# A diffusion layer on one core: context values and the bias on ScalarE's queue, value stores a step late, router sums over eight units

## The chip, the cores and the metric

The kernel runs on one core of one Trainium2 chip. The metric is the device time of one execution in microseconds (us), as the median over runs. The core has five engines that work side by side, each through its own list of instructions in order: TensorE (PE, its weight loads listed as PEld), VectorE (DVE), ScalarE (ACT), GpSimd (POOL) and SyncE (SP). SP does nothing but ask for transfers. In this kernel nearly all transfers are asked for on SP's queue; the other engines' queues can do it too, and then the requests stand in order among that engine's own instructions.

## What is computed

One layer for 1024 latent tokens of width 1024 and 256 context tokens. The input projection feeds three groups of heads: neighbourhood attention (8 heads of 64), a two-way linear recurrence (LRU, 256 channels) and a gated short convolution (256 channels). Each group is normalised, all go through one output projection, and a mixture of 16 experts follows.

```python
...
u = h @ w_in
uc = hc @ w_in[:, c_lo:c_hi]
...
# neighbourhood attention, one row of the grid, 4 groups of 16 queries, 8 rows x 32 columns of keys and the context
s_loc = jnp.einsum('bnqhd,brnkhd->bhnqrk', qr, kb) * scale + bias     # masked to the window
s_ctx = jnp.einsum('bnqhd,bchd->bhnqc', qr, kc) * scale
p = jax.nn.softmax(jnp.concatenate([s_loc, s_ctx], -1), axis=-1)
out = p_loc @ vb + p_ctx @ vc
...
y = jnp.concatenate([rms_norm(y_na, g0), rms_norm(y_lru, g1), rms_norm(y_sc, g2)], -1) @ w_out
x = x + mod[:, 2] * y
h = modulate(rms_norm(x, norm_ffn_g), mod[:, 3], mod[:, 4])
x = x + mod[:, 5] * moe_ffn(h)          # router: softmax(h @ w_router + b_router), top-2 within a group
return rms_norm(x, final_g)
```

`mod` are six rows of 1024 numbers, silu(c) @ w_ada + b_ada.

## The kernel before

All matrix products are made of two or three products of rounded parts: a number is split into a high and a low part (`hi` by a copy on ScalarE, `lo` by a subtraction on VectorE).

**Input projection** (`inproj`). The 22 blocks of 128 output columns are taken in the order of `CHUNKS`: LRU and convolution inputs, the gates, then values (blocks 10 to 13), keys (14 to 17) and queries (18 to 21). A block has two groups of 512 tokens, and blocks of keys, values and LRU inputs a third of 256 context tokens; a group is 24 matmuls (L334). Other work runs between them as Python generators in two lists, `side` and `late`: after the first half of a group `pump(side)` lets each task of `side` go on to its next `yield`, after the second half, `pump(side, late)` does it for both. A `yield` is thus the distance of one step, and what a task issues between two yields is written at that place into every engine's list. Tasks that the change touches:

- `norm` (L457 to L496), twice (convolution, then LRU): squares on ScalarE (L463), their sum on GpSimd (L464), two yields, then the sum over channels by matmuls with a column of ones into `pm` (L469), a root (L471, L472), a broadcast by matmuls (L478), scaling on VectorE (L482), splitting (L489 makes the low part) and four stores to `y_d` in device memory. `gelu` (L448 to L454) makes its input.
- `mod_rows` (from L504), four passes `p`, for the modulation rows 2 to 5: eight loads of `w_ada` (`mw`), summed on VectorE into `macc` (L518, then L520), a split (L526 on GpSimd makes the low part into `mw`), one yield, and four matmuls per pass with a column of ones (L532).
- `ev_v` for the values: it transposes a group's `vT` on PE (L622), copies the high part from PSUM into one of three buffers (L627, ScalarE), subtracts for the low part (L628, VectorE) and asks SP for the store to `v_d`.

**Attention** has 32 units `u` (4 column groups of 8 heads) of two halves `g`. Per half: scores by four matmuls (L760), bias addition and row maximum in one instruction on VectorE (L764), exponential (L772, ScalarE), five transposes (L783), a copy for the high part (L785) and a subtraction (L786) for the low part, then the value matmuls L810 of the unit before, over 13 jobs: 5 in the first half, 8 in the second. `vw[0..3]` are rows of the latent values (`block<-v_d`, `values_rows`), `vc` the context values. The bias tables `bt` (two buffers, for two heads each) come from `b_d` by two loads per pair of heads, then GpSimd adds the mask in two instructions (L723); `bias(p)` does pair `p`, with pair 0 before attention.

**Router weights.** `wout_step(u)` at u = 24 multiplies and sums eight columns of `wr` into `sws` (L958, then seven L960) and folds the row into `wr` (L961).

What orders the work: the order of the source lines, the two generator lists, and the order on SP's queue.

Of the kernel before, what the change touches and what calls it, by code (L numbers as in the profile page):

```python
# [8 lines left out]
F32 = mybir.dt.float32  # L9
# [9 lines left out]
P = 128  # L19
# [52 lines left out]
class Kernel:  # L72
# [291 lines left out]
    def inproj(self, hc_es):  # L364
# [93 lines left out]
        def norm(ys, base):  # L458
# [3 lines left out]
            for ch in range(2):  # L462
                S.activation(sq[ch][:, 0:T], ys[ch][:, 0:T], AF.Square)  # L463
            G.tensor_add(out=sq[0][:, 0:T], in0=sq[0][:, 0:T], in1=sq[1][:, 0:T])  # L464
            yield 1
            yield 1
            pn = self.pmm.tile([P, 8], F32, name="pm")
            for t in range(8):
                E.matmul(pn[:, t:t + 1], sq[0][:, t * P:(t + 1) * P], ones[:, 0:1], start=True, stop=True)  # L469
# [28 lines left out]
        def mod_rows():  # L498

            def get(q):  # L500
                if q < 4 * KD:
                    p, k = divmod(q, KD)
                    wa = self.mo.tile([P, D], F32, name="mw", bufs=2)
                    self.load(wa, a["w_ada"][k * P:(k + 1) * P, (p + 2) * D:(p + 3) * D])  # L504
                    was.append(wa)
            was = []
            get(0)
            one = self.mo.tile([P, 1], F32R, name="one", bufs=1)
            S.copy(one, ones[:, 0:1])
            for p in range(4):  # L510
                acc = self.mo.tile([P, D], F32, name="macc")
                row = self.mo.tile([1, D], F32, name="mrow")
                self.load(row, a["b_row"][:, (p + 2) * D:(p + 3) * D])
                for k in range(KD):
                    get(p * KD + k + 1)
                    wa = was.pop(0)
                    if k == 0:
                        V.tensor_scalar_mul(acc, wa, self.sil[:, 0:1])  # L518
                    else:
                        V.scalar_tensor_tensor(out=acc, in0=wa, scalar=self.sil[:, k:k + 1], in1=acc, op0=ALU.mult, op1=ALU.add)  # L520
                    if k != 1:
                        yield 1
                hi = self.vp.tile([P, D], F32R, name="mhi", bufs=1)
                S.copy(hi, acc)
                lo = self.mo.tile([P, D], F32R, name="mw", bufs=2)
                G.tensor_sub(out=lo, in0=acc, in1=hi.bitcast(F32))  # L526
                yield 1
                for hh in range(2):
                    cs = slice(hh * 512, hh * 512 + 512)
                    pr = self.psu.tile([P, 512], F32, name="ps")  # L530
                    for i, x in enumerate((hi, lo)):
                        E.matmul(pr[0:1, :], one, x[:, cs], start=(i == 0), stop=(i == 1))  # L532
                    V.tensor_add(row[:, cs], pr[0:1, :], row[:, cs])
                self.load(self.mod_d[p:p + 1, :], row)
                yield 1
# [76 lines left out]
            side.append(gelu(ch, x))  # L612
        side.append(norm(ylru, 0))

        def ev_v(ch):
            pend = []

            def transposes():
                o, n, vT = pend.pop()
                pt = self.pst.tile([P, 512], F32, name="pt")  # L620
                for i in range(n // P):
# [4 lines left out]
                pv = pt[:, 0:n].rearrange("p (b d) -> p b d", d=64)  # L626
                S.copy(vo[:, 0:2 * nb, 0, :], pv)  # L627
                V.tensor_sub(vo[:, 0:2 * nb, 1, :], pv, vo[:, 0:2 * nb, 0, :].bitcast(F32))  # L628
                self.load(self.v_d[o:o + n, 2 * ch:2 * ch + 2].rearrange("(b p) h j d -> p b (h j d)", p=P),
                          vo[:, 0:2 * nb].rearrange("p (b h) j d -> p b (h j d)", h=2).bitcast(F32))  # L630

            def ev(g, o, n, ps):
                if pend:
# [8 lines left out]
        for ch in range(4):  # L642
# [8 lines left out]
            block(10 + ch, evac)  # L651
            flush = fl
        flush()
        drain(side)
        gp_es.close()

# [56 lines left out]
        for g in range(2):  # L713
            self.load(self.masks[n][:, g], self.a["mask"][3 * g + TY[n]])

    def bias(self, p):

        n, h, bt = p // 4, 2 * (p % 4), self.bts[p % 2]
        for g in range(2):
            o = (128, 0)[g]  # L720
            v = bass.AP(tensor=bt.tensor, offset=bt[:, g, 0:1].offset, ap=[list(bt.ap[0]), [640, 2], [1, 384]])
            self.load(v, self.b_d[h:h + 2, TY[n], :, o:o + 384].rearrange("h p k -> p h k"))
            self.G.tensor_add(out=v, in0=v, in1=self.masks[n][:, g:g + 1].to_broadcast([P, 2, 384]))  # L723

    def values_rows(self, n, u):
# [8 lines left out]
    def attention(self):  # L734
# [9 lines left out]
        with self.pool("ap") as ap:  # L744
# [43 lines left out]
            def values(u, part):  # L788
                n, h = divmod(u, 8)
                vw = vws[n]  # L790
                if part == 0:
# [3 lines left out]

                jobs = [(vc[:, 0, h], 3, 3), (vc[:, 1, h], 4, 4), (vw[1][:, h], 1, 0), (vw[2][:, h], 2, 1),
                        (vw[0][:, h], 0, None), (vw[3][:, h], None, 2)]
                jobs = [(ph, P) + j for j in jobs[2:] + jobs[:1]] + [(pl, 64) + j for j in jobs] + [(ph, P) + jobs[1]]
                for q, (pp, m, w, b0, b1) in enumerate(jobs):
                    if (q >= 5) != part:  # L800
                        continue
# [52 lines left out]
                for j in range(2):  # L854
                    self.load(self.y_d[j][2 * n + g, :, 0:4], yn[j].bitcast(F32))

            self.load(vc.bitcast(F32), self.v_d[T:TA].rearrange("(b p) h j d -> p b h (j d)", p=P))
            self.bias(1)
            self.load(grow, a["mg"][:, 0:512].to_broadcast([P, 512]))
            last = 32  # L860
            for g in range(2):
# [43 lines left out]
    def wout_step(self, u):  # L905
# [36 lines left out]
        if u == 31:  # L942
# [8 lines left out]
            self.mix_load(1, [self.kq[i] for i in (12, 13, 14)])  # L951
            self.slot = op.tile([P, P], F32, name="slot")
            self.load(self.slot, a["slot"].to_broadcast([P, P]))
        if u == 24:
            V, cols, wr = self.V, self.cols, self.wr

            V.scalar_tensor_tensor(out=cols[1], in0=cols[1], scalar=1.0, in1=cols[2], op0=ALU.add, op1=ALU.mult)
            V.tensor_scalar_mul(self.sws, wr[:, 0, :], cols[0][:, 0:1])  # L958
            for k in range(1, KD):
                V.scalar_tensor_tensor(out=self.sws, in0=wr[:, k, :], scalar=cols[0][:, k:k + 1], in1=self.sws, op0=ALU.mult, op1=ALU.add)  # L960
            V.tensor_tensor(out=wr, in0=wr, in1=cols[1][:, :, None].to_broadcast([P, KD, NE]), op=ALU.mult)  # L961

    def mix_load(self, it, bufs=None):
# [871 lines left out]
```

## Time and profile before

| | us |
|---|---|
| median of 3 runs (lowest, highest) | 1130.27 (1129.08, 1131.17) |
| the profiled execution | 1134.46 |
| its span on the core | 1132.5 |
| PE busy | 1020.2 (90%) |
| PEld busy | 836.5 (74%) |
| VectorE busy | 825.3 (73%) |
| ScalarE busy | 592.1 (52%) |
| GpSimd busy | 307.9 (27%) |

251.21 MB move, 222 GB/s on average, and the mean granted clock is 0.96. The input projection lasts until about 392 us, attention until about 565, the output projection and the router until about 700, the experts until the end. A row of the timeline gives the start and the length, then engine, line, operation, what it writes and reads, shapes and count (several equal neighbours in one row), and in brackets how long the engine had been idle before it and what ended this. For SP the length is the time of asking, not that of the transfer.

### The profile page before, as it was taken

How to read it: one execution, taken by the hardware profiler on the slowest of the kernel's cores; microseconds unless marked ns; L12 is line 12 of the kernel's file. 1: busy time of each engine (PE TensorE's matmuls, PEld its weight loads, DVE VectorE, ACT ScalarE, POOL GpSimd, SP SyncE). 2: the span in 40 equal slices, each digit the busy share in tenths (PEclk: the TensorE clock that was granted, in tenths of full speed). 3: DMA queues.
4: the chain of work that ended last, by engine and by line, in shares of the span. 5: the costliest groups of instructions: out<-in, count | busy, mean ns of one | idle time of the engine just before them, and what ended most of it. 6: DMA issues, size and time to landing. Idle time of an engine off the chain costs nothing. (4 is left out here: it accounts for less than half of the span.)

```text
span 1132.5 us, 15754 instructions
## 1 busy us (share of the span) xinstructions
PE 1020.2 (90%) x5242; PEld 836.5 (74%) x5243; DVE 825.3 (73%) x1415; ACT 592.1 (52%) x964; POOL 307.9 (27%) x212
## 2 busy tenths in 40 slices
PE   2699999998999979998799997699999999999994
PEld 2587777786888779897678886577777777777773
DVE  5876898644553358887667776879898979788965
ACT  6565673431233258786522223556565757566751
POOL 3630011310001034344303224131423233231432
PEclk9879999998999989998999997899999999999997
DMA  9441434878624676774776856978989989898873
GB/s 330 125 121 60 133 96 116 277 259 258 208 85 116 146 217 179 213 213 129 266 249 215 295 156 228 343 275 251 337 271 310 289 274 323 242 350 241 300 242 138
DMA packets 139595, 251.21 MB, mean 222 GB/s; under 512 B 25283, under 2 KB 87205, under 8 KB 139460
## 3 DMA queue, kind: packets, MB, share of 16 engines
q1 hardware_dynamic: 131620, 229.97, 61.9%
q0 software_dynamic: 6736, 19.53, 7.4%
q8 instruction: 45, 0.74, 0.3%
q10 hardware_dynamic: 1152, 0.63, 0.2%
q14 instruction: 42, 0.34, 0.1%
HBM read 211.94 MB, written 45.55 MB: 227 GB/s over the span
## 5 line engine op out<-in xcount | busy, mean ns | idle before, releaser
L334 PE MATMUL ps<-h,block 128*128 128x512 f32 x1056 | 258.8, 403 | 2.8 <-DVE block L321 1.8
L334 PEld LDWEIGHTS ps<-h,block 128*128 128x128 f32 x1056 | 201.6, 194 | 45.0 <-DVE block L321 2.6
L1367 PE MATMUL pg<-q,xT 128*128 128x512 f32 x448 | 137.3, 399 | 3.4 <-DVE xT L93 2.7
L1367 PE MATMUL pg<-k,xT 128*128 128x512 f32 x320 | 113.2, 408 | 3.9 <-PEq L1578 3.7
L1323 POOL DMA_INDIRECT acc_d<-yt,recs x15 | 69.3, 4620 | 125.4 <-DVE yt L1392 125.4
L1367 PEld LDWEIGHTS pg<-q,xT 128*128 128x128 f32 x448 | 84.9, 190 | 24.6 <-DVE xT L93 2.8
L1743 DVE TENSOR_TENSOR q<-block,k 128x1024 fp32r<-128x1024 f32 x80 | 94.9, 1218 | 2.7 <-ACT k L1742 1.8
L1387 PE MATMUL py<-k,hT 128*128 128x512 f32 x204 | 81.1, 435 | 10.3 <-DVE hT L1379 4.2
L1742 ACT CAST k<-block 128x1024 fp32r<-128x1024 f32 x80 | 80.2, 1047 | 3.7 <-DMA recs<-list_d 3.4
L723 POOL TENSOR_TENSOR bt<-bt,mask 128x768 f32<-128x768 f32 x32 | 59.0, 1859 | 81.8 <-DMA bt<-b_d 61.1
L1367 PEld LDWEIGHTS pg<-k,xT 128*128 128x128 f32 x320 | 61.7, 193 | 18.5 <-issue 3.8
L772 ACT ACTIVATE sm<-sm,mx 128x640 f32<-128x640 f32 x64 | 53.2, 832 | 26.6 <-DVE mx L764 26.5
L786 DVE TENSOR_TENSOR p<-ps,p 128x640 fp32r<-128x640 f32 x64 | 52.6, 822 | 16.1 <-ACT p L785 16.1
L520 DVE SCALAR_TENSOR_TENSOR macc<-mw,sil,macc 128x1024 f32<-128x1024 f32 x28 | 40.7, 1455 | 28.4 <-DMA mw<-in_w_ada_dram 28.2
L783 PE MATMUL ps<-cst,sm 128*128 128x128 f32 x320 | 49.6, 289 | 12.9 <-DVE mx L764 12.0
L1387 PEld LDWEIGHTS py<-k,hT 128*128 128x128 f32 x204 | 39.6, 194 | 28.0 <-DVE hT L1379 10.7
L764 DVE CUSTOM_DVE_ANT_0 sm<-ps,bt 128x640 f32<-128x640 f32 x64 | 52.2, 818 | 9.9 <-POOL bt L723 7.1
L760 PE MATMUL ps<-k,q 128*128 128x384 f32 (+1 forms) x256 | 53.8, 335 | 4.0 <-DVE yn L93 2.3
L1284 POOL DMA_INDIRECT block<-h_d,recs x21 | 27.1, 1292 | 96.3 <-PE pt L1333 87.3
L785 ACT CAST p<-ps 128x640 fp32r<-128x640 f32 x64 | 44.3, 692 | 14.9 <-PE ps L783 14.4
L783 PEld LDWEIGHTS ps<-cst,sm 128*128 128x128 f32 x320 | 38.3, 149 | 16.0 <-issue 12.7
L760 PEld LDWEIGHTS ps<-k,q 128*128 128x128 f32 x256 | 44.6, 200 | 5.9 <-DVE yn L93 2.5
(373 smaller groups left out, 2293.9 us busy)
## 6 DMA issues: line engine op xcount, KB each, us to landing
block<-in_w_moe_dram SPq DMA_DIRECT2D x120, 512.0 KB
raw<-in_w_moe_dram SPq DMA_DIRECT2D x36, 512.0 KB
mw<-in_w_ada_dram SPq DMA_DIRECT2D x32, 512.0 KB
bt<-b_d SPq DMA_DIRECT2D x32, 384.0 KB
k<-in_w_moe_dram SPq DMA_DIRECT2D x24, 512.0 KB
block<-in_w_in_dram SPq DMA_DIRECT2D x22, 512.0 KB
wa<-in_w_ada_dram SPq DMA_DIRECT2D x16, 512.0 KB
block<-v_d SPq DMA_DIRECT2D x64, 128.0 KB
```

Source lines behind the costliest of these rows:

```text
L334: self.E.matmul(ps[:, 0:n], l[:, k, :], r[:, m, :], start=(k == 0 and q == 0), stop=(k == KD - 1 and q == 2))
L723: self.G.tensor_add(out=v, in0=v, in1=self.masks[n][:, g:g + 1].to_broadcast([P, 2, 384]))
L760: E.matmul(ps[:, dst], self.qs[i][h][:, it * P:(it + 1) * P], kv, start=(i == 0), stop=(i == 1))
L764: V.tensor_tensor_reduce(out=sm, in0=ps[:, all_], in1=self.bts[(u // 2) % 2][:, g, b0:b0 + 640], op0=ALU.add, op1=ALU.min, scale=-1.0, sca ...
L772: S.activation(sms[u, g], sms[u, g], AF.Exp, scale=-1.0, bias=mx, accum_out=lss[n][:, g, h:h + 1])
L783: E.transpose(pt[:, b * P:(b + 1) * P], sm[:, c:c + P], ident)
L786: return lambda: V.tensor_sub(pl, pt, ph.bitcast(F32))
L1323: nc.gpsimd.indirect_dma_start(out=acc_d, out_offset=bass.IndirectOffsetOnAxis(ap=rec[0:m, 1:2], axis=0), in_=y[0:m], in_offset=None, comp ...
L1367: E.matmul(self.pg[half], self.xT[x][:, k, :], self.w.gu(k, m, half), start=(k == 0 and i == 0), stop=(k == KD - 1 and i == 2))
L1387: E.matmul(self.py[c], hTs[x][:, f, :], self.w.dn(f, m, c), start=(f == 0 and i == 0), stop=(f == 3 and i == 2))
L1742: k.S.copy(hi, raw)
L1743: (eng or k.V).tensor_sub(lo, raw, hi.bitcast(F32))
```

## The change

Six edits:

1. `norm` has three yields, not two, ahead of the matmuls with ones.
2. `mod_rows` has one more yield between the split and the row matmuls, in each of four passes.
3. `ev_v` keeps a value store back in `done` and asks for it when the next tile has been copied; the last is asked for after the last tile.
4. At the start of attention, `bias(1)` is asked for first and then `vc`, both on ScalarE's queue; before, SP was asked for `vc`, then `bias(1)`.
5. The value jobs are in another order: the first half has the four latent ones with the high part and the first with the low part, the context ones all come in the second half.
6. The eight sums of `sws` are asked for one each in units 17 to 24; the two other instructions stay at u = 24.

Line numbers of the changed kernel are 1 larger from L527, and up to 13 larger behind.

```diff
@@ norm
-            yield 1
-            yield 1
+            for _ in range(3):
+                yield 1
@@ mod_rows
                 G.tensor_sub(out=lo, in0=acc, in1=hi.bitcast(F32))
                 yield 1
+                yield 1
@@ inproj
+        done = []
+
+        def store():
+
+            while done:
+                self.load(*done.pop())
+
@@ ev_v
-                self.load(self.v_d[o:o + n, 2 * ch:2 * ch + 2].rearrange("(b p) h j d -> p b (h j d)", p=P),
-                          vo[:, 0:2 * nb].rearrange("p (b h) j d -> p b (h j d)", h=2).bitcast(F32))
+                store()
+                done.append((self.v_d[o:o + n, 2 * ch:2 * ch + 2].rearrange("(b p) h j d -> p b (h j d)", p=P),
+                             vo[:, 0:2 * nb].rearrange("p (b h) j d -> p b (h j d)", h=2).bitcast(F32)))
@@ inproj, behind the blocks of values
         flush()
+        store()
@@ bias
-            self.load(v, self.b_d[h:h + 2, TY[n], :, o:o + 384].rearrange("h p k -> p h k"))
+            self.load(v, self.b_d[h:h + 2, TY[n], :, o:o + 384].rearrange("h p k -> p h k"), eng)
@@ values
-                jobs = [(ph, P) + j for j in jobs[2:] + jobs[:1]] + [(pl, 64) + j for j in jobs] + [(ph, P) + jobs[1]]
+                jobs = [(ph, P) + j for j in jobs[2:]] + [(pl, 64) + j for j in jobs[2:] + jobs[:2]] + [(ph, P) + j for j in jobs[:2]]
@@ attention
-            self.load(vc.bitcast(F32), self.v_d[T:TA].rearrange("(b p) h j d -> p b h (j d)", p=P))
-            self.bias(1)
+            self.bias(1, S)
+            self.load(vc.bitcast(F32), self.v_d[T:TA].rearrange("(b p) h j d -> p b h (j d)", p=P), S)
@@ wout_step
+        if 17 <= u < 25:
+            V, k, s = self.V, u - 17, self.cols[0][:, u - 17:u - 16]
+            if k == 0:
+                V.tensor_scalar_mul(self.sws, self.wr[:, k, :], s)
+            else:
+                V.scalar_tensor_tensor(out=self.sws, in0=self.wr[:, k, :], scalar=s, in1=self.sws, op0=ALU.mult, op1=ALU.add)
@@ wout_step, u == 24
-            V.tensor_scalar_mul(self.sws, wr[:, 0, :], cols[0][:, 0:1])
-            for k in range(1, KD):
-                V.scalar_tensor_tensor(out=self.sws, in0=wr[:, k, :], scalar=cols[0][:, k:k + 1], in1=self.sws, op0=ALU.mult, op1=ALU.add)
```

The first place at which the order on an engine differs is VectorE in the first block of values, while the LRU norm runs. `g_816`, `g_817` and `g_822` are tiles of values (L628 is L636 in the changed kernel), L482 and L489 the norm's, `macc` the modulation row, L321 a weight split. Before:

```order
L482 SCALAR_TENSOR_TENSOR g_823<-g_823,vt,ps 128x512
L482 SCALAR_TENSOR_TENSOR g_821<-g_821,vt,ps 128x512
L520 SCALAR_TENSOR_TENSOR macc<-mw,sil,macc 128x1024 x2
L489 TENSOR_TENSOR g_825<-g_823,g_818 128x8x4x16
L489 TENSOR_TENSOR g_819<-g_821,g_815 128x8x4x16
L628 TENSOR_TENSOR g_816<-pt,g_816 128x8x64
L520 SCALAR_TENSOR_TENSOR macc<-mw,sil,macc 128x1024
L628 TENSOR_TENSOR g_817<-pt,g_817 128x8x64
L520 SCALAR_TENSOR_TENSOR macc<-mw,sil,macc 128x1024
L321 SCALAR_TENSOR_TENSOR block_2005<-block_1872,block_2004 128x1024
L628 TENSOR_TENSOR g_822<-pt,g_822 128x4x64
```

On the same engine at the same place in the changed kernel:

```order
L482 SCALAR_TENSOR_TENSOR g_823<-g_823,vt,ps 128x512
L482 SCALAR_TENSOR_TENSOR g_821<-g_821,vt,ps 128x512
L636 TENSOR_TENSOR g_816<-pt,g_816 128x8x64
L489 TENSOR_TENSOR g_825<-g_823,g_818 128x8x4x16
L489 TENSOR_TENSOR g_819<-g_821,g_815 128x8x4x16
L518 TENSOR_SCALAR macc<-mw,sil 128x1024
L636 TENSOR_TENSOR g_817<-pt,g_817 128x8x64
L520 SCALAR_TENSOR_TENSOR macc<-mw,sil,macc 128x1024 x2
L321 SCALAR_TENSOR_TENSOR block_1998<-block_1852,block_1997 128x1024
L636 TENSOR_TENSOR g_822<-pt,g_822 128x4x64
```

The pair of L520 that stood between L482 and L489 is gone from there; the pass of the row begins (L518) behind L489, and a pair of L520 stands ahead of the third tile's subtraction.

The second place is the start of attention: SP before, from the last rows of values (`block_2900`) on, and ScalarE in the changed kernel. DMAHW0 to DMAHW7 are eight counters of finished transfers that all requests use in turn; a request waits until the one before it on its counter has landed. Before, on SP:

```order
L84 DMA block_2900<-v_d 32x1024 [waits DMAHW7_49]
L84 DMA q_2661<-q_2661 64x1024 [waits DMAHW0_49,Activation_49]
L84 DMA q_2669<-q_2669 64x1024 [waits DMAHW1_49,DVE_49]
L84 DMA q_2662<-q_2662 64x1024 [waits DMAHW2_49,Activation_49]
L84 DMA q_2670<-q_2670 64x1024 [waits DMAHW3_49,DVE_49]
L84 DMA vc<-v_d 128x2x1024 [waits DMAHW4_49,PE_49]
L84 DMA bt_2978<-b_d 128x2x384 [waits DMAHW5_49,PE_49]
L84 DMA bt_2978<-b_d 128x2x384 [waits DMAHW6_49]
L84 DMA grow<-in_mg_dram 128x512 [waits DMAHW7_49]
```

On ScalarE in the changed kernel, and, in the second fence, on SP:

```order
L702 CAST q_2661<-ps 64x8x4x16 [waits PE_49]
L702 CAST q_2662<-ps 64x8x4x16 [waits DVE_49]
L84 DMA bt_2978<-b_d 128x2x384 [waits DMAHW4_49]
L84 DMA bt_2978<-b_d 128x2x384 [waits DMAHW6_49]
L84 DMA vc<-v_d 128x2x1024 [waits DMAHW0_49]
L782 ACTIVATE sm,ls<-sm,mx 128x640 [waits DVE_49] x2
```

```order
L84 DMA block_2895<-v_d 32x1024 [waits DMAHW3_49,PE_49]
L84 DMA block_2895<-v_d 32x1024 [waits DMAHW4_49]
L84 DMA block_2895<-v_d 32x1024 [waits DMAHW5_49]
L84 DMA block_2895<-v_d 32x1024 [waits DMAHW6_49]
L84 DMA block_2900<-v_d 32x1024 [waits DMAHW7_49,PE_49]
L84 DMA block_2900<-v_d 32x1024 [waits DMAHW0_49]
L84 DMA block_2900<-v_d 32x1024 [waits DMAHW1_49]
L84 DMA block_2900<-v_d 32x1024 [waits DMAHW2_49]
L84 DMA q_2661<-q_2661 64x1024 [waits DMAHW3_49,Activation_49]
L84 DMA q_2669<-q_2669 64x1024 [waits DMAHW4_49,DVE_49]
```

The three requests stand on ScalarE behind its last copy of queries and ahead of its first exponential (L782 is L772 before). Counters 4, 6 and 0, which they take, are counters of loads of value rows on SP's queue too.

The third place is VectorE at the end of units 23 and 24 (L969, L973 and L974 are L960, L957 and L961 before). Before, behind the last subtraction of unit 24:

```order
L786 TENSOR_TENSOR p_4495<-ps,p_4494 128x640
L957 SCALAR_TENSOR_TENSOR vt<-vt 128x8
L958 TENSOR_SCALAR vt<-vec,vt 128x16
L960 SCALAR_TENSOR_TENSOR vt<-vec,vt 128x16 x7
L961 TENSOR_TENSOR vec<-vec,vt 128x128
```

In the changed kernel:

```order
L969 SCALAR_TENSOR_TENSOR vt<-vec,vt 128x16
L774 ISA sm,mx<-ps,bt_2674 128x640
L774 ISA mx 128x1
L796 TENSOR_TENSOR p_4502<-ps,p_4501 128x640
L774 ISA sm,mx<-ps,bt_2674 128x640
L774 ISA mx 128x1
L796 TENSOR_TENSOR p_4502<-ps,p_4501 128x640
L969 SCALAR_TENSOR_TENSOR vt<-vec,vt 128x16
L973 SCALAR_TENSOR_TENSOR vt<-vt 128x8
L974 TENSOR_TENSOR vec<-vec,vt 128x128
```

Three operations are left at the end of unit 24, and one stands at the end of each of the seven units before.

## Rows read from the trace of the kernel before

**Rows 1.** What PE waited for, 110 to 400 us: total us, times, longest

```profile
PE pt L622 <- DVE g L628: 5.5, 1, 5.5
PE pm L469 <- POOL g L464: 3.1, 2, 2.3
PE ps L532 <- POOL mw L526: 1.4, 1, 1.4
```

**Rows 2.** Stretches: us, busy PE PEld DVE ACT POOL, clock, DMA share, GB/s

```profile
270.00:273.00 3.00, 0.28 (x2) 0.31 (x3) 3.00 (x4) 0.00 (x0) 0.00 (x0) 0.56 1.07 372
392.00:412.00 20.00, 10.62 (x58) 9.92 (x57) 8.99 (x18) 8.12 (x16) 5.90 (x5) 0.79 1.04 278
412.00:515.00 103.00, 99.94 (x801) 96.63 (x801) 83.10 (x162) 83.38 (x173) 44.75 (x27) 0.99 0.69 191
```

**Rows 3.** Timeline, second norm, 213 to 231 us

```profile
213.68 1.22 DVE L454 SCALAR_TENSOR_TENSOR g<-g,g 128x1024 f32<-128x1024 f32 x1
...
223.53 2.40 POOL L526 TENSOR_TENSOR mw<-macc,mhi 128x1024 fp32r<-128x1024 f32 x1 [2.17 <-DMA y_d<-g]
223.75 3.26 DVE L454 SCALAR_TENSOR_TENSOR g<-g,g 128x1024 f32<-128x1024 f32 x1
...
227.05 1.06 ACT L463 ACTIVATE g<-g 128x1024 f32<-128x1024 f32 x1 [2.69 <-DVE g L454]
```

**Rows 4.** Timelines of VectorE, SP and PE, values blocks, 250 to 287 us

```profile
250.69 1.28 DVE L520 SCALAR_TENSOR_TENSOR macc<-mw,sil,macc 128x1024 f32<-128x1024 f32 x1 [5.69 <-DMA mw<-in_w_ada_dram]
...
255.33 1.28 DVE L489 TENSOR_TENSOR g<-g,g 128x512 fp32r<-128x512 f32 x2
...
257.75 5.05 SPq L84 DMA_DIRECT2D y_d<-g  x4
263.24 1.41 SPq L84 DMA_DIRECT2D mw<-in_w_ada_dram  x1
...
269.82 1.28 DVE L520 SCALAR_TENSOR_TENSOR macc<-mw,sil,macc 128x1024 f32<-128x1024 f32 x1 [10.81 <-DMA mw<-in_w_ada_dram]
...
273.46 7.46 PE L334 MATMUL ps<-h,block 128*128 128x512 f32 x24
...
280.89 5.72 PE L334 MATMUL ps<-h,block 128*128 128x512 f32 x24
```

**Rows 5.** Timeline, start of attention, 395 to 410 us

```profile
395.58 0.83 ACT L772 ACTIVATE sm<-sm,mx 128x640 f32<-128x640 f32 x1 [1.62 <-DVE mx L764]
...
397.31 1.05 SPq L84 DMA_DIRECT2D vc<-v_d  x1
398.46 1.60 SPq L84 DMA_DIRECT2D bt<-b_d  x2
...
405.55 0.39 PE L810 MATMUL pv<-p,vc 128*128 128x256 f32 x1 [3.93 <-DMA vc<-v_d]
...
406.62 7.13 POOL L723 TENSOR_TENSOR bt<-bt,mask 128x768 f32<-128x768 f32 x4 [13.96 <-DMA bt<-b_d]
...
409.43 1.30 PE L783 MATMUL ps<-cst,sm 128*128 128x128 f32 x5 [2.91 <-DVE mx L764]
```

**Rows 6.** Timelines of VectorE and PE, two units in the run, 416 to 423 us

```profile
416.97 0.82 DVE L786 TENSOR_TENSOR p<-ps,p 128x640 fp32r<-128x640 f32 x1 [0.44 <-ACT p L785]
...
418.35 0.33 PE L810 MATMUL pv<-p,vc 128*128 128x256 f32 x1
...
422.41 0.33 PE L810 MATMUL pv<-p,vc 128*128 128x256 f32 x1
```

**Rows 7.** Unit 24: VectorE's tile vt (ns: least, median, most), and the timeline, 515 to 523

```profile
L960 DVE SCALAR_TENSOR_TENSOR vt<-vec,vt x7: 235/235/1765, 516.1 to 520.7; 128x16 f32<-128x16 f32 x7
...
515.96 1.83 POOL L723 TENSOR_TENSOR bt<-bt,mask 128x768 f32<-128x768 f32 x1 [0.79 <-DVE vt L957]
516.07 4.90 DVE L960 SCALAR_TENSOR_TENSOR vt<-vec,vt 128x16 f32<-128x16 f32 x7
...
522.19 1.30 PE L783 MATMUL ps<-cst,sm 128*128 128x128 f32 x5 [4.43 <-DVE mx L764]
```

More of the change, by code (lines that the diff above doesn't have):

```diff
@@ L714, in mask, with bias @@
             self.load(self.masks[n][:, g], self.a["mask"][3 * g + TY[n]])
-    def bias(self, p):
+    def bias(self, p, eng=None):
         n, h, bt = p // 4, 2 * (p % 4), self.bts[p % 2]
```

## The prediction

> **What bounds the kernel now.** I read the page first: TensorE (PE) is busy 90% of the span, so most of the 1130 us are matmuls that this change doesn't touch, and only places where PE stands still can give time back. I then listed what PE waited for up to the start of attention, looked at the order of time around each of those waits, and did the same for the first microseconds of attention and for unit 24, the two other places that the diff names.
>
> In the input projection PE's longest wait is 5.5 us at the transposes of the values (L622) on VectorE (DVE); next come the ones-matmuls of the two group norms (L469), 3.1 us together and 2.3 in the second, and the row matmuls L532, 1.4 [rows 1]. From 392 to 412 us PE is busy 10.62 of 20 us while the DMA engines are full (share 1.04) [rows 2]. Between 412 and 515 us attention runs well: PE 99.94 of 103 us, with DVE at 83.10 and GpSimd (POOL) at 44.75 [rows 2]. At the end of unit 24 PE stands still once more, for 4.43 us [rows 7].
>
> The sum is made against the profiled execution, 1134.46 us (span 1132.5 and 2.0 around it). That execution is 4.2 us above the median of the runs, 1130.27; I assume that it holds the same waits and carry the difference over to the median. A measurement of this kernel can tell about 0.2% (2.3 us) from no change.
>
> **The change part by part.** A step of the front is one call of the pump between two groups of matmuls; a group of 24 lasts 5.72 us at full clock [rows 4].
>
> *A, first norm.* Of the 3.1 us at L469, 2.3 belong to the second norm, so 0.8 to the first [rows 1]. An added yield puts a whole group of matmuls ahead of it: **-0.8** (bounds -0.8 and 0).
>
> *B, second norm and the row matmuls.* Here GpSimd's L526 (from 223.53, 2.40 us) and DVE's L454 (from 223.75) run side by side, and L454 takes 3.26 us; the one before it, with GpSimd idle, took 1.22 at 213.68 [rows 3]. So ScalarE's square waits 2.69 us for L454 and begins at 227.05, GpSimd's sum follows, and PE waits 2.3 us; the matmuls L532 wait 1.4 us for the same L526 [rows 1, 3]. With one more yield in each pass of the row task, this L526 (of the second pass) lies one step later, behind the norm's own sum on POOL, and L532 and L469 each come a step later than their input. All of it would be -3.7. I take **-2.4**: L526 now queues on POOL behind the norm's sum, so I leave 1.3 us, most of the 1.4 of L532, as it is. Bounds -3.7 and 0.
>
> *C, the clock after it.* After the 5.5 us wait at L622 the same 24 matmuls took 7.46 us instead of 5.72, so a pause costs 1.74 more at a lower granted clock [rows 4]. B's pauses together are 3.7 us; I take half of that price, **-0.9** (bounds -1.74 and 0).
>
> *D, the stall at the values.* The chain ends in DVE's L520, the step-by-step sum of a modulation row: it waited 10.81 us for its load, until 269.82, and L628, which PE wants, stands behind it on DVE. The load was issued at 263.24 because four y_d stores held SP's queue from 257.75 for 5.05 us; and they were late because the L489 that fills them ran at 255.33, behind L520s, the first of which began at 250.69 after 5.69 us of waiting for its load [rows 4]. In the changed order no L520 stands between L482 and L489, so the stores can go when the norm is done, up to 10 us sooner (255.33 - 250.69 + 5.69 = 10.3), and the load behind them as well; 5.5 us sooner is enough to remove the wait. The value stores, now asked for a step late, no longer hold SP until DVE has finished the tile that they read; their number is unchanged, and they cost nothing: values are read again more than 100 us later. The third buffer covers the longer hold; if it did not, ScalarE's copy into it would wait, and PE with it. D's whole is 5.5 + 1.74 = -7.2. L520 still stands ahead of the tile's subtraction, and its loads still share the DMA engines with the stores, so I leave 1.9 us: **-5.3** (bounds -7.2 and 0).
>
> *E, start of attention.* The vc load takes SP 1.05 us from 397.31 and the two bias loads 1.60 from 398.46. PE waits 3.93 us for vc, then the bias add on POOL waits 13.96 for its loads, and PE waits 2.91 more behind DVE's L764 [rows 5]. With the bias first and on ScalarE's queue it is issued about 4 us sooner, more than 2.91, so that wait goes: **-2.9**. The 3.93 I keep: vc is wanted later now, by the reordered jobs, but the value rows of the first tile are wanted in its place, and these stand on SP's queue, in the same full DMA engines, some of them behind completion counters that the new issues on ScalarE now share. ScalarE issues three DMAs (2.65 us in all by the SP rows) ahead of its exponentials; it had 1.62 us idle before one [rows 5], so at most 1.0 of them is felt, and I put that to the lower gain. Bounds -6.8 (both waits) and 0.
>
> *The order of the value jobs* puts a matmul with the low part of the probabilities into the first half. It needs DVE's L786 of the half before, which in the unit shown runs 416.97 to 417.79, and the first value matmul starts at 418.35 [rows 6]: cover 0.5 us, cost **0**. Without cover a late L786 would hold PE by up to its 0.82 in a unit.
>
> *F, router sums.* Seven L960 take 4.90 us: the longest runs 1.76 us, beside GpSimd's bias add (1.83), against 0.235 as a rule, and 4.90 holds two of the long kind and five short ones; PE waits 4.43 us behind them [rows 7]. Taken from unit 24, they leave the two last operations, which the same bias add can still hold once, 1.5 us (1.76 - 0.235): saved 4.9 - 1.5 = 3.4. Each of the eight spread operations can meet a bias add: POOL is busy 44.75 of 103 us, so 3.5 of eight do, each 1.5 us against the DVE slack of a unit, which lasts 4.06 us (418.35 to 422.41 [rows 6]): (103 - 83.1) / 103 x 4.06 = 0.8: 3.5 x 0.7 = 2.5 given back. Less half the clock price, 0.9: -3.4 + 2.5 - 0.9 = **-1.8**. Bounds: all of the wait and its clock, -4.43 - 1.74 = -6.2; all eight held, 8 x 0.7 - 3.4 = +2.2.
> The Trainium skill, "SBUF — State Buffer", section "Who interferes with whom", says that a VectorE instruction with two SBUF inputs contends with a GpSimd instruction that reads SBUF, and that of two that want the shared port pair the second "fully blocks". The trace agrees in two of seven, 1.76 against 0.235 us; that rule speaks against spreading, and carries rival 1.
>
> **Sum:** -0.8 - 2.4 - 0.9 - 5.3 - 2.9 - 1.8 = -14.1. 1134.46 - 14.1 = 1120.4 in the profiled execution's terms, 1130.27 - 14.1 = **1116.2 us** for the median.
>
> **The rivals.**
> 1. *The spread sums are held in every unit.* Each of the two L960 that met an add was held for most of it. If POOL's adds meet all eight, F is +2.2 instead of -1.8, 4.0 worse: 1120.2. For it: GpSimd is busy 0.43 of the time, in pieces of 1.83 us, so a hold is often a long one. Against it: DVE has 0.8 us a unit free.
> 2. *Everything goes.* The stall, its clock and both waits at the start of attention vanish: -0.8 - 3.7 - 1.7 - 7.2 - 6.8 - 6.2 = -26.4; the front's clock is never quite back, so I price it at -24: 1106. For it: each is a wait for an order, not for work. Against it: 1.04 of DMA share at 392 to 412.
> 3. *The waits are DMA capacity, not order.* In 270 to 273 us the DMA engines were full (1.07, 372 GB/s) with PE at 0.28 of 3 us [rows 2]. Then D and E stay: -14.1 + 5.3 + 2.9 = -5.9, 1124.4. Against it: SP's four stores held the load back by 5.05 us whatever the bandwidth.
> 4. *Slower: the sum's loads are late at more places.* The row task is spread over four more steps; its L520 stand on DVE ahead of the transposes' subtraction, which PE needs. A wait for a load is hidden while it is shorter than the 5.72 us of a group; beyond that PE stands. If two other sums of these rows meet a wait as long as the 10.81, while the first stays, D is +14.4 instead of -5.3: -14.1 + 5.3 + 14.4 = +5.6, **1135.9**. Against it: the stores go earlier, and no other wait of 5.5 us stands in the list.
>
> **How the numbers follow.** The forecast 0.48, rival 1 0.17, rival 2 0.13, rival 3 0.14, rival 4 0.08. The forecast's own range, with its terms off by a third each, is 1110 to 1123. The range leaves out rival 4, half of rival 2 and a little of rival 3, together under 0.2: **1105 to 1126**. Faster by over 0.2% is below 1128.0: the forecast, rivals 1 and 2 and most of 3, 0.87; within 0.2%, the rest of 3 with a little of 4, 0.05; slower 0.08.
>
> **What would show it.** A right: no wait at the first L469. B right: L454 at 1.2 us beside no L526, and L532 without its 1.4. D right: no wait over 2 us at L622's place, the next 24 matmuls near 5.72 us, y_d stores issued near 247. E right: the bias add begins by 403, PE's wait behind L764 gone, and one near 4 us on value rows. F right: no run of seven sums, single ones of 1.8 us where an add is under way, and a PE wait at unit 24 below 1.5. What would make the prediction wrong: the big stall standing with another wait behind it, or units 17 to 24 longer than 4.06 us each by more than 0.5.

## Result, and the profile after

The changed kernel took 1117.97 us (median of 5 runs, 1112.07 to 1120.49) beside 1129.87 for the kernel before: ratio 0.9889, 95% interval 0.9867 to 0.9911, so 10 to 15 us faster. A second comparison, later, gave 1118.24 and 0.9886 (0.9851 to 0.9920). The prediction was 1116.2 us.

Its profiled execution was the fastest of the five, 1112.07 us, span 1110.3, granted clock 0.977; that of before, 1134.46, is longer than each of its five timed runs (up to 1131.17). The two are thus further apart than the medians, and a second profiled execution of the changed kernel, 1117.81 us and so near its median, stands beside the first as *again*. To see where the time went I therefore compare stretches, from the start of one group of PE instructions to that of another, in every kernel that was profiled. *Gate* is the first matmul of the recurrence's gates, *T4* and *T9* the fourth and ninth groups of value transposes (L622), *att* the first scores, *u1*, *u22*, *u26*, *u32* the first L821 of the back-transposes of that unit, by count. All numbers are us.

| stretch | before | after | again | yields alone | stores alone | attention alone | sums alone |
|---|---|---|---|---|---|---|---|
| start to gate | 104.40 | 100.86 | 100.61 | 100.81 | 101.08 | 103.36 | 103.34 |
| gate to T4 (terms A to C) | 144.49 | 144.70 | 145.79 | 144.56 | 144.97 | 144.11 | 144.19 |
| T4 to T9 (D) | 31.87 | 24.16 | 24.30 | 26.64 | 24.04 | 31.99 | 32.10 |
| T9 to att | 111.09 | 111.17 | 111.14 | 111.17 | 111.24 | 111.13 | 111.12 |
| att to u1 (E) | 22.61 | 20.61 | 21.37 | 22.26 | 23.29 | 19.65 | 22.75 |
| u1 to u22 | 93.97 | 94.65 | 95.07 | 94.29 | 94.00 | 94.58 | 95.38 |
| u22 to u26 (F) | 22.82 | 16.53 | 16.57 | 22.44 | 23.12 | 22.25 | 16.46 |
| u26 to u32 | 30.92 | 30.07 | 31.76 | 30.71 | 30.12 | 30.61 | 31.98 |
| u32 to the end | 570.33 | 567.55 | 569.49 | 567.72 | 568.74 | 567.52 | 568.58 |

Of the 22.2 us between the two spans, 3.5 lie ahead of the gates and 2.8 behind attention, where no edit is; they go with the execution, not with the change. What is left, 15.9 us, is D (-7.7), F (-6.3, with +0.7 and -0.9 in the units around it), E (-2.0), and nothing from A to C (+0.2). The second execution leaves 11.8 us, close to the 12.5 of the ratio: D -7.6, F -6.3 with +1.1 and +0.8 around it, E -1.2, A to C +1.3. D and F thus repeat within 0.2 us. A to C, E and the units around F differ by 0.4 to 1.7 us between these two executions of one kernel, and a difference of that size in a single profile shows nothing.

What PE waited for, 110 to 400 us, in the changed kernel (total us, times, longest):

```profile
PE pv L820 <- DMA block<-v_d: 5.1, 2, 3.3
PE pt L630 <- ACT vT L645: 4.6, 2, 3.6
PE ps L770 <- DVE q L703: 2.2, 1, 2.2
...
PE pm L469 <- POOL g L464: 0.8, 1, 0.8
```

Beside [rows 1], the 5.5 us at the transposes, the 1.4 at L532 and the first norm's wait are gone, and the second norm's 2.3 us are down to 0.8. In their place stands a wait of 3.6 us at a transpose (L630 is L622 before) behind ScalarE's copy. The timeline shows where it comes from:

```profile
212.61 10.34 SPq L84 DMA_DIRECT2D y_d<-g  x4
...
223.06 1.06 ACT L463 ACTIVATE g<-g 128x1024 f32<-128x1024 f32 x1 [4.66 <-DMA y_d<-g]
...
224.49 0.59 ACT L645 COPY vT<-ps 128x512 f32<-128x512 f32 x1
...
225.13 0.66 PE L630 MATMUL pt<-cst,vT 128*128 128x128 f32 x4 [3.63 <-ACT vT L645]
226.50 2.36 POOL L526 TENSOR_TENSOR mw<-macc,mhi 128x1024 fp32r<-128x1024 f32 x1
226.60 3.57 PE L469 MATMUL pm<-ones,g 128*128 128x1 f32 x16 [0.81 <-POOL g L464]
```

ScalarE's second square (L463) writes into a buffer which a store of the first norm still reads. It waits 4.66 us, and the copy that PE needs stands behind it. The matmuls L469 then take 3.57 us, at a granted clock of 0.50 (the 1.2 GHz level) from 226.6 to 230.2 us; before, the clock fell in the same way behind the second norm's wait, to 0.53 from 232.6 to 236.0. The big stall is gone: the y_d stores are asked for from 247.82, 2.3 us behind T4 (before from 257.75, 8.9 behind T4), and a wait of L520 for its load no longer reaches PE, though it still lasts 8.92 us. The 24 matmuls take 5.71 us at a granted clock of 1.00 (2.4 GHz); before they took 7.46, the first 4 us of it at 0.53 [rows 4].

```profile
247.82 4.52 SPq L84 DMA_DIRECT2D y_d<-g  x4
...
260.89 1.28 DVE L520 SCALAR_TENSOR_TENSOR macc<-mw,sil,macc 128x1024 f32<-128x1024 f32 x1 [8.92 <-DMA mw<-in_w_ada_dram]
...
263.79 0.63 PE L630 MATMUL pt<-cst,vT 128*128 128x128 f32 x4
264.17 5.71 PE L334 MATMUL ps<-h,block 128*128 128x512 f32 x24
265.75 0.59 ACT L635 CAST g<-pt 128x512 fp32r<-128x512 f32 x1 [3.60 <-DMA v_d<-g]
```

The last row is a price of the late stores that the prediction ruled out with "The third buffer covers the longer hold": ScalarE's copy of a tile waits 3.60 us for a value store that still reads its buffer, and no such wait stands in the profile of before. Here PE doesn't feel it, since its next transposes begin at 269.72.

At the start of attention, in the order of time (SP rows, ScalarE's requests as ACTq, and the two waits of PE):

```profile
379.05 1.50 SPq L84 DMA_DIRECT2D block<-v_d  x3
382.43 0.91 ACTq L84 DMA_DIRECT2D bt<-b_d  x2
383.38 0.48 ACTq L84 DMA_DIRECT2D vc<-v_d  x1
385.89 1.86 SPq L84 DMA_DIRECT2D block<-v_d  x4
385.94 3.63 POOL L733 TENSOR_TENSOR bt<-bt,mask 128x768 f32<-128x768 f32 x2 [4.23 <-DMA bt<-b_d]
391.61 1.23 SPq L84 DMA_DIRECT2D block<-v_d  x3
393.24 0.41 PE L820 MATMUL pv<-p,block 128*128 128x256 f32 x2 [3.28 <-DMA block<-v_d]
395.45 0.66 PE L820 MATMUL pv<-p,block 128*128 128x128 f32 x2 [1.79 <-DMA block<-v_d]
```

The bias add begins 5.1 us behind the first scores (380.89) instead of 14.8 (406.62 against 391.85), and PE no longer waits for it. But SP asks for no row between 380.6 and 385.9, nor from 387.8 to 391.6. What SP waited for, 373 to 400 us, and the windows in which it did (columns as in [rows 2]):

```profile
SPq L84 <- DMA bt<-b_d: 5.6, 2, 5.3
SPq L84 <- DMA vc<-v_d: 3.9, 1, 3.9
```

```profile
381.00:385.00 4.00, 1.76 (x12) 1.59 (x11) 2.36 (x5) 1.53 (x3) 0.53 (x1) 1.00 0.45 131
385.00:389.00 4.00, 2.92 (x21) 2.41 (x19) 3.03 (x8) 3.58 (x8) 3.06 (x2) 1.00 1.00 352
389.00:393.00 4.00, 0.96 (x8) 0.69 (x6) 2.26 (x4) 2.40 (x5) 0.57 (x1) 1.00 0.70 173
```

SP's loads of value rows wait for the very transfers that were moved to ScalarE's queue, through the counters that both use, and the share of the DMA engines falls to 0.45 and 0.70. PE then waits 5.1 us for rows, where it waited 3.9 for context values.

The router sums (the tile vt: least, median, most ns; and the one that was held):

```profile
L969 DVE SCALAR_TENSOR_TENSOR vt<-vec,vt x7: 224/226/1110, 476.3 to 503.6; 128x16 f32<-128x16 f32 x7
...
498.64 1.84 POOL L733 TENSOR_TENSOR bt<-bt,mask 128x768 f32<-128x768 f32 x1 [3.31 <-DMA bt<-b_d]
499.41 1.11 DVE L969 SCALAR_TENSOR_TENSOR vt<-vec,vt 128x16 f32<-128x16 f32 x1
```

One of eight met a bias add in this execution, and the two that stay at the end of unit 24 met none; in the second execution two of eight did (1.83 and 1.14 us). The 4.43 us of [rows 7] are gone; of PE's waits for that instruction of VectorE there are left, between 470 and 515 us,

```profile
PE ps L793 <- DVE mx L774: 1.0, 3, 0.4
```

### The profile page after: what moved, and what is told of

It is laid out like the page before. It is cut to its first block, busy times and chain, and to the rows that moved or that the text cites. A ratio compares the mean times of both kernels' runs of the same rounds, so it can differ in the third digit from the quotient of the medians.

```text
span 1110.3 us, 15751 instructions
## 1 busy us (share of the span) xinstructions
PE 1006.4 (91%) x5242; PEld 821.0 (74%) x5243; DVE 820.9 (74%) x1415; ACT 592.5 (53%) x964; POOL 305.5 (28%) x212
## 5 line engine op out<-in xcount | busy, mean ns | idle before, releaser
L334 PE MATMUL ps<-h,block 128*128 128x512 f32 x1056 | 255.6, 398 | 2.1 <-DVE block L321 1.2
L334 PEld LDWEIGHTS ps<-h,block 128*128 128x128 f32 x1056 | 198.7, 191 | 44.1 <-DVE block L321 2.2
L782 ACT ACTIVATE sm<-sm,mx 128x640 f32<-128x640 f32 x64 | 53.2, 831 | 19.5 <-DVE mx L774 19.1
L793 PE MATMUL ps<-cst,sm 128*128 128x128 f32 x320 | 47.0, 278 | 7.6 <-DVE mx L774 6.8
L520 DVE SCALAR_TENSOR_TENSOR macc<-mw,sil,macc 128x1024 f32<-128x1024 f32 x28 | 37.7, 1347 | 20.8 <-DMA mw<-in_w_ada_dram 20.6
L98 POOL TENSOR_TENSOR ms<-ms,cst 128x1 f32<-128x1 f32 x26 | 17.5, 679 | 105.4 <-DVE ms L97 85.4
```

The costliest lines, as they stand in the source:

```text
L334: self.E.matmul(ps[:, 0:n], l[:, k, :], r[:, m, :], start=(k == 0 and q == 0), stop=(k == KD - 1 and q == 2))
L782: S.activation(sms[u, g], sms[u, g], AF.Exp, scale=-1.0, bias=mx, accum_out=lss[n][:, g, h:h + 1])
L793: E.transpose(pt[:, b * P:(b + 1) * P], sm[:, c:c + P], ident)
```

## The experiments

**Each part alone**, on the kernel before.

Yields (edits 1 and 2):

```diff
-            yield 1
-            yield 1
+            for _ in range(3):
+                yield 1
...
+                yield 1
```

> The kernel before with the added yields alone (both norms and the row matmuls). Theory: these move the pairs of L520 away from the norm's L489, so the y_d stores go sooner and the 5.5 us wait of PE at the transposes of the values goes, with some 2 us of clock; the first norm gives 1 to 2 us; the second norm gives nothing, because ScalarE's second square then waits for the landing of a y_d store of the first norm. Sum -7 to -8 us, about 1122.5. Rival: the late value stores are what frees the queue; then the yields alone give 2 us or less, 1128 or more, and the wait of over 4 us stays.

Measured: 1126.45 us, ratio 0.9989 (0.9974 to 1.0003): between the two forecasts, and not told from no change. Its profile shows the theory's picture: gate to T4 144.56 us as before, with ScalarE waiting for a store, and the big stall cut from 5.54 to 2.43 us:

```profile
266.09 0.63 PE L623 MATMUL pt<-cst,vT 128*128 128x128 f32 x4 [2.43 <-DVE g L629]
266.47 5.70 PE L334 MATMUL ps<-h,block 128*128 128x512 f32 x24
```

T4 to T9 is 5.2 us shorter, yet the ratio gives 1.2. The profiled execution, 1122.39, is the fastest of its 12 runs (up to 1129.40); how long the stall is in the others no trace tells, and this stays open.

Stores (edit 3):

```diff
-                self.load(self.v_d[o:o + n, 2 * ch:2 * ch + 2].rearrange("(b p) h j d -> p b (h j d)", p=P),
...
+                store()
+                done.append((self.v_d[o:o + n, 2 * ch:2 * ch + 2].rearrange("(b p) h j d -> p b (h j d)", p=P),
...
```

> The kernel before with the value stores asked for a step late, alone. Theory: the order of L520 and L489 on VectorE is that of before, so the y_d stores start as late as before and the 5.5 us wait stays: within 1.5 us of 1130. Rival: the value stores held SP's queue ahead of the loads of the row sums; then the wait shrinks by 3 us or more and the time falls to 1126 or below.

Measured: 1121.87 us, ratio 0.9938 (0.9918 to 0.9958). The rival won: the stall is gone, with L520 and L489 on VectorE in the order of before. What held the load stands among SP's own waits, here the three longest. Before, 247 to 266 us, then with late stores, 240 to 260:

```profile
SPq L84 <- DVE g L628: 4.8, 1, 4.8
SPq L84 <- DMA mw<-in_w_ada_dram: 2.7, 1, 2.7
SPq L84 <- DVE g L482: 2.1, 1, 2.1
```

```profile
SPq L84 <- DVE g L489: 3.3, 1, 3.3
SPq L84 <- DVE g L635: 3.0, 1, 3.0
SPq L84 <- DVE macc L520: 2.7, 2, 1.3
```

Before, SP stood 4.8 us at a value store until L628 was done, with the y_d stores and the load of the row sum behind it. Counted from T4, that load was asked for at 14.4 us (263.24 - 248.89) before and at 8.5 (254.53 - 246.05) with late stores. The gain repeats: T4 to T9 lasts 24.04 to 24.31 us in eight profiles with late stores, and 31.87 to 32.10 in the three with neither these nor the yields; two variants below, with another buffer, are longer.

Start of attention (edits 4 and 5, of which these are the lines that ask for the loads):

```diff
-            self.load(vc.bitcast(F32), self.v_d[T:TA].rearrange("(b p) h j d -> p b h (j d)", p=P))
-            self.bias(1)
+            self.bias(1, S)
+            self.load(vc.bitcast(F32), self.v_d[T:TA].rearrange("(b p) h j d -> p b h (j d)", p=P), S)
```

> The kernel before with the start of attention alone: bias and context values on ScalarE's queue and the new order of the value jobs. Theory: the wait behind the bias add (2.9 us) goes, the 3.9 us for context values is replaced by one of 4 to 5 us for the rows of values: -1 to -3 us, 1127 to 1129. Rival: both waits go, -5 us or more, 1125 or below.

Measured: 1127.32 us, ratio 0.9988 (0.9968 to 1.0008), in the theory's range, not told from no change; att to u1 is 3.0 us shorter.

Router sums (edit 6, whose lines stand in the change):

> The kernel before with the router sums over eight units, alone. Theory after seeing the changed kernel: one sum of the seven met a bias add, for 1.1 us, so the whole stall of unit 24 with its clock goes, -5 to -6.5 us, about 1124.5. Rival, as forecast: GpSimd's adds hold several of the sums, and it gives 2 us or less, 1128 or more.

Measured: 1126.42 us, ratio 0.9965 (0.9949 to 0.9982), about 4 us, between the two forecasts. The stall goes whole (-6.4 from u22 to u26), and some 1 to 2 us come back in the units before and behind. Two of the eight sums were held by a bias add, one for 1.74 us and one for 0.88:

```profile
L959 DVE SCALAR_TENSOR_TENSOR vt<-vec,vt x7: 223/225/1736, 488.0 to 516.2; 128x16 f32<-128x16 f32 x7
...
512.14 0.88 DVE L959 SCALAR_TENSOR_TENSOR vt<-vec,vt 128x16 f32<-128x16 f32 x1
```

The four parts add up to 0.11 + 0.62 + 0.12 + 0.35 = 1.20%, against 1.11% for the whole (interval 0.89 to 1.33). The sum alone doesn't show that they are independent: by the profiles the yields and the stores shorten the same stall. Only the stores and the sums are told from no change by the time.

**What the yields do beside the late stores.** Without them:

```diff
-            for _ in range(3):
-                yield 1
+            yield 1
+            yield 1
...
-                yield 1
```

> The changed kernel without the added yields (norms and row matmuls as before). Theory: the yields save nothing once the value stores are late: what they take from the first norm (some 2 us) they lose to ScalarE's wait for a y_d store in the second, and the 5.5 us wait is removed by the late stores alone. Then this kernel is within 2 us of the changed one, 1116 to 1120. Rival: the yields carry their part as forecast, 4 us; then it is slower, 1121 or more.

Measured: 1114.83 us, ratio 0.9882 (0.9861 to 0.9904): not slower than the changed kernel, so the rival's 4 us are excluded. Gate to T4 takes 144.94 us, T4 to T9 24.04. Beside the late stores the yields bring nothing that can be measured.

A free buffer for the second square:

```diff
-            sq = [free.pop(0) for _ in ys]
+            sq = [free.pop(0), free.pop(0 if base else 2)]
```

> The changed kernel with one difference: in the second norm the second square goes into a buffer of the list that no store is reading. Theory: the new 3.6 us wait of PE at the transposes behind ScalarE's copy is the wait of ScalarE's square for a y_d store of the first norm; it goes, PE gains 3 to 5 us with the clock, 1113 to 1115. Rival: ScalarE is late for another reason (GpSimd's gelu product, or DVE), and the wait stays within 1 us: 1117 or more.

Measured: 1115.40 us, ratio 0.9877 (0.9860 to 0.9894). The wait for the store is gone (ScalarE now waits 2.73 us for L454) and gate to T4 falls to 141.22 us, 3.5 less than in the changed kernel: the cause was the buffer. T4 to T9 then grows by 1.9 to 26.01: PE is 3.5 us sooner at T4, but the load of L520 lands only 1.6 us sooner (L520 begins at 259.28 instead of 260.89), and PE waits at the transposes behind it:

```profile
221.16 1.06 ACT L463 ACTIVATE g<-g 128x1024 f32<-128x1024 f32 x1 [2.73 <-DVE g L454]
...
223.23 0.66 PE L630 MATMUL pt<-cst,vT 128*128 128x128 f32 x4 [1.70 <-ACT vT L645]
...
262.18 0.63 PE L630 MATMUL pt<-cst,vT 128*128 128x128 f32 x4 [1.78 <-DVE g L636]
```

**The start of attention.** The three loads on GpSimd's queue:

```diff
-            self.bias(1, S)
-            self.load(vc.bitcast(F32), self.v_d[T:TA].rearrange("(b p) h j d -> p b h (j d)", p=P), S)
+            self.bias(1, G)
+            self.load(vc.bitcast(F32), self.v_d[T:TA].rearrange("(b p) h j d -> p b h (j d)", p=P), G)
+            self.bias_add(1)
```

> The changed kernel with the two bias loads and the context values asked for on GpSimd's queue (both loads ahead of the two adds). Theory: on ScalarE they take completion counters amid SP's loads of value rows, and SP stood still 5.6 us for the bias and 3.9 for the context values while the DMA engines fell to a share of 0.56 and 0.65; on GpSimd's queue they have counters of their own, SP asks for its rows without a gap, PE's 5.1 us on value rows shrinks to 2 or less: 3 us faster, 1114 to 1116. Rival: the DMA engines are the limit there; PE's wait only moves to another tile, within 1.5 us of the changed kernel.

Measured: 1114.53 us, ratio 0.9884 (0.9858 to 0.9909), by the ratio the same as the changed kernel. SP no longer waits for these loads, so the eight counters are not shared by all requests, as the text on the change has it, but by those of SP and ScalarE. PE no longer waits for rows, but it now waits for the context values, with the DMA engines full all the while (share 1.01 to 1.05):

```profile
PE pv L828 <- DMA vc<-v_d: 5.0, 1, 5.0
```

```profile
384.00:388.00 4.00, 2.93 (x21) 2.49 (x20) 2.96 (x6) 3.78 (x8) 0.53 (x1) 1.00 1.04 293
388.00:392.00 4.00, 3.15 (x25) 2.69 (x23) 3.37 (x9) 3.04 (x6) 3.08 (x2) 1.00 1.05 279
392.00:396.00 4.00, 0.00 (x0) 0.00 (x0) 0.69 (x1) 0.00 (x0) 0.00 (x0) 0.62 1.01 257
```

So the pause at the counters was real and yet cost less than can be told: the wait moved to another tile, as the rival says, which speaks for the capacity of the DMA engines as the limit here. The stretch att to u1 takes 19.95 us against 20.61 and 21.37, but seven profiles with the same start of attention have 18.71 to 22.18, so this stretch alone decides nothing.

Context values back on SP:

```diff
-            self.load(vc.bitcast(F32), self.v_d[T:TA].rearrange("(b p) h j d -> p b h (j d)", p=P), S)
+            self.load(vc.bitcast(F32), self.v_d[T:TA].rearrange("(b p) h j d -> p b h (j d)", p=P))
```

> The changed kernel with the context values back on SP's queue behind the moves of queries, the bias still first on ScalarE's. Theory: SP no longer stands still for the context values (3.9 us), only for the bias (5.6); the last value rows land some 4 us sooner and the context values, wanted last, are still in time: 1 to 3 us faster, 1115 to 1117. Rival: the context values are then the late ones, PE waits for them as in the kernel before (3.9 us): same or slower, 1118 to 1120.

Measured: 1116.77 us, ratio 0.9891 (0.9873 to 0.9908). The picture is the rival's, though the time can't be told from the changed kernel's: PE waits 6.5 us for context values, and att to u1 takes 22.73 us, about as before the change. In these kernels PE waits for what comes last: context values before, rows in the changed kernel, context values again here.

```profile
PE pv L820 <- DMA vc<-v_d: 6.5, 1, 6.5
```

**The last four**, on one chip.

The changed kernel once more:

> The changed kernel itself once more, beside the three others of this call. Both theories: 1116 to 1119.

Measured: 1118.24 us, ratio 0.9886 (0.9851 to 0.9920). Its profile is the column *again*.

The added yield in the first norm alone:

```diff
-            for _ in range(3):
+            for _ in range(3 if base else 2):
...
-                yield 1
```

> The changed kernel with the added yield in the first norm alone (second norm and row matmuls as before). Theory: the first norm's 2 us stay and the second norm's new wait for a y_d store does not come, so the stretch from the first gate matmuls to the fourth transposes takes 142.5 to 143.5 us instead of 144.7: 1 to 2 us faster than the changed kernel. Rival: with the first norm later, its y_d stores land later whatever the second norm does, and ScalarE waits for them as in the changed kernel: the stretch stays over 144 us.

Measured: 1117.97 us, ratio 0.9895 (0.9865 to 0.9924). The rival won: gate to T4 takes 147.78 us. The wait for the store is there with the first norm alone later, so it doesn't come from what the second does (without any added yield ScalarE waits for L454 instead, 2.73 us):

```profile
224.15 1.06 ACT L463 ACTIVATE g<-g 128x1024 f32<-128x1024 f32 x1 [4.74 <-DMA y_d<-g]
```

The free buffer, without the added yield of the row matmuls:

```diff
-            sq = [free.pop(0) for _ in ys]
+            sq = [free.pop(0), free.pop(0 if base else 2)]
...
-                yield 1
```

> The changed kernel without the added yield of the row matmuls, and with the second square in a buffer that no store reads. Theory: ScalarE doesn't wait for a store, L526 again runs beside VectorE's L454 and holds it, as in the kernel before; the stretch to the fourth transposes takes 142 to 143 us, and the later one to the ninth some 24 (its loads are asked for as early as with the late stores alone): 2 to 3 us faster than the changed kernel. Rival: PE, earlier by then, meets the load of the row sum again, as it did for 1.8 us with the new buffer alone: no more than 1.5 us faster.

Measured: 1116.58 us, ratio 0.9890 (0.9860 to 0.9920). Gate to T4 falls to 141.47 as the theory says, but T4 to T9 grows to 28.71, and by the ratio nothing is gained, as the rival says. The cause is the rival's in part only: of the two waits of PE at the transposes the shorter, 1.60 us, goes back to L520 and its load, but the longer, 2.62, stands behind a copy on ScalarE which had waited 9.03 us for a value store that still read its buffer. Here the price of the late stores reaches PE:

```profile
263.53 0.58 ACT L634 CAST g<-pt 128x512 fp32r<-128x512 f32 x1 [9.03 <-DMA v_d<-g]
...
264.65 0.66 PE L629 MATMUL pt<-cst,vT 128*128 128x128 f32 x4 [2.62 <-ACT vT L644]
```

The value jobs in the order of before:

```diff
-                jobs = [(ph, P) + j for j in jobs[2:]] + [(pl, 64) + j for j in jobs[2:] + jobs[:2]] + [(ph, P) + j for j in jobs[:2]]
+                jobs = [(ph, P) + j for j in jobs[2:] + jobs[:1]] + [(pl, 64) + j for j in jobs] + [(ph, P) + jobs[1]]
```

> The changed kernel with the value jobs in the order of before (context values in both halves, the first low part in the second half). Theory: the order itself costs and brings nothing once the units run (within 0.7 us from the first to the 22nd unit); at the start of attention PE waits for value rows as before, since they land last: within 1 us of the changed kernel. Rival: the order is what lets PE run on while the last rows come; then the first unit ends 2 us later or more.

Measured: 1117.21 us, ratio 0.9888 (0.9859 to 0.9918). u1 to u22 takes 94.76 us against 94.65, att to u1 20.23 against 20.61: the order of the jobs costs and brings nothing that these profiles can tell. In this execution no sum was held, but the last operation of unit 24, otherwise 0.29 us, met a bias add, and u22 to u26 takes 18.09 us instead of 16.53:

```profile
505.70 1.95 DVE L974 TENSOR_TENSOR vec<-vec,vt 128x128 f32<-128x128 f32 x1
```

None of the seven variants can be told from the changed kernel; the intervals of all overlap.

## Why the prediction was right, and where its steps were not

The time came out near the forecast, -12.5 us by the ratio against -14.1. The places were right, but the sum is in part luck: A to C gave nothing and F gave more than was priced. The measured numbers are those of the two profiled executions.

- **A, B, C: -4.1 forecast, nothing measured (+0.2 and +1.3).** A came (up to the first transposes PE is 2.1 us sooner, 0.8 of it the wait that A names). B's signs came too, L454 at 1.22 us and no wait at L532, but its step "L532 and L469 each come a step later than their input" left out what else a later first norm delays: its y_d stores, asked for 111.8 us behind the gate instead of 108.7, and with them the buffer that the second square writes. Of 3.7 us of waits 2.9 went, and one of 3.6 us came, with the clock falling behind it as it did before; so C gave nothing either. With another buffer the stretch is 3.5 us shorter, but 1.9 of it are lost again at the next load.
- **D: -5.3 forecast, -7.7 and -7.6 measured, by another way.** The stall and its clock were the right thing to price, and the bound of -7.2 was passed by 0.5. The step "they were late because the L489 that fills them ran at 255.33, behind L520s" is wrong as the deciding cause: late stores alone remove the stall in that very order. SP stood at a value store for 4.8 us. The order of L520 and L489 is not without effect: the yields alone cut T4 to T9 by 5.2 us in their one profile, though the time by only 0.11%. The prediction said that value stores would no longer hold SP, but gave the credit to the yields; SP's own waits would have told. Its sign, y_d stores near 247, could not tell the two apart: with late stores alone they begin at 247.75. That the third buffer covers the longer hold is wrong, with 3.60 us of waiting on ScalarE that PE happens not to feel.
- **E: -2.9 forecast, -2.0 and -1.2 measured, as told.** The wait for the bias went, and one for value rows came in place of the one for context values, with SP held at the shared counters. Over all profiles att to u1 lasts 22.7 us on average in the four without edits 4 and 5, and 20.6 in the seven with both as they are. Rival 3 is wrong for D. Here it has a part: E did not stay at nothing, but with SP free and the DMA engines full the remaining wait only moved.
- **F: -1.8 forecast, -6.3 at unit 24 and up to 2 us back in the units around it.** Both sides were mis-sized. Unit 24 gave the whole of the bound (-6.2), where the sum had kept 1.5 us for a hold at its end and half of the clock's price; of ten profiles with spread sums one has such a hold (1.95 us). And "3.5 of eight do" is too many: none to two did in each of the ten, 13 of 80 in all, and such a sum took 0.9 to 1.9 us in place of 0.22. GpSimd's share of time, 0.43, is thus not the chance of a meeting. That both have their place in a unit may be why; no run tested it. The rule of the Trainium skill, "SBUF — State Buffer", section "Who interferes with whom", says that a VectorE instruction with two SBUF inputs contends with a GpSimd instruction that reads SBUF. The trace agrees (1.11 us against 0.226, beside a GpSimd add of 1.84), but the rule does not tell how often they meet. Rival 1 fell.
- **The value jobs: 0 forecast, 0 measured** (0.1 us from u1 to u22).
- **Rivals 2 and 4.** The front did not give everything, and no wait came up at more places behind the row sums. Rival 4's premise, that PE stands when a load is late by more than the 5.72 us of a group, is wrong: L520 waited 8.92 us and PE did not.

## What to carry to other kernels

Read the waits of the queue that asks for transfers beside those of the engines: here a store that waited for its data held every load behind it, and asking for it one step later alone gave 0.62% of the 1.11%. When work is moved later, look up who next writes the buffers it frees: the later norm held a square, and the later value store a copy. At the start of attention, where the DMA engines were full, the wait moved to whichever transfer came last; fewer bytes there, or bytes brought earlier, would be the next thing to try (not tried). And a sign that two mechanisms would both give confirms neither.

## What was not expected

The kernel's runs spread by some 8 us, and the longer ones have the lower granted clock: 1112.07 us at 0.977, 1115.73 at 0.970, 1120.49 at 0.964. A part of it arises ahead of any edit, at the start, where PE has many short pauses. The same eight transposes took 1.95 us at a granted clock of 0.50 in the profile of before and 1.07 at 1.00 in that of the changed kernel, and PE reached the gates between 99.78 and 104.40 us in the fourteen profiles. Rows of before, then of after:

```profile
60.08 1.95 PE L251 MATMUL pt<-cst,x 128*128 128x128 f32 x8
```

```profile
57.96 1.07 PE L251 MATMUL pt<-cst,x 128*128 128x128 f32 x8
```
